# Seven products for eight in three more projections of a two-layer decoder trunk

## The chip, the cores and the metric

The kernel runs as one program on one core of a Trainium2 chip. The metric is the time of one execution on the device, in microseconds (us): the median of several runs. A profiled execution, taken apart, gives the trace.

## The reference, cut to what matters

256 tokens with 2048 features go through two layers. Each layer adds three things to the residual `h`: a mixer, a gated MLP and a gated embedding.

```python
for i in range(DEPTH):                      # 2 layers
    hn = rms_norm(h, mixer_norm[i])
    h = h + (mla_mixer if i == 0 else gdn_mixer)(hn, ...)
    gate, up = split(rms_norm(h, ffn_norm[i]) @ w_gate_up[i])      # 2048 -> 2 x 5632
    h = h + (silu(gate) * up) @ w_down[i]                          # 5632 -> 2048
    e = rms_norm(p[i] @ w_proj[i], ple_norm[i])                    # 256 -> 2048
    h = h + e * sigmoid(rms_norm(h, ple_gate_norm[i]) @ w_gate[i]) # 2048 -> 2048
...
# gdn_mixer (DeltaNet): proj = hn @ w_in, 2048 -> 12352: q 2048, k 2048, v 4096, z 4096, b 32, a 32
#   q, k, v = silu(conv4(...)); q, k l2-normed per head; a chunked gated delta rule per value head
#   (triangular solve inside a chunk, a state carried over the chunks); o = rms_norm(o) * silu(z); o @ w_out
```

All tensors are float32.

## The kernel before

**Tiling.** The 256 tokens are two row tiles (T = 2) of 128. A matrix product runs over blocks of 512 output columns and over k-tiles of 128 input features. The activations stand transposed in SBUF, one k-tile of one row tile being the 128x128 stationary operand; the weights stream past it, 512 columns at a time, into a PSUM bank.

**Precision.** TensorE takes a shortened float32 (F32R). So each operand is split in two: the high part, which is a cast, and the remainder. `products` (lines 312 to 316) issues three matmuls for each product: high x high, high x remainder of the weight, remainder of the activation x high. The remainder of a weight tile is made at run time by `wsplit` (lines 104 to 111): ScalarE casts `raw` to `wh` (L109), VectorE subtracts (`wl`, L110). A weight tile is 128 x (4 k-tiles x 512).

**Buffers.** `wtile` (lines 90 to 97) hands out the weight tiles: three each of `raw`, `wh` and `wl`, and in the FFN two more `raw`, one more `wh` and `wl` from the pool `extra`. A tile takes one whole buffer however much of it is used. Four PSUM banks (`psmm`) hold accumulators of the large products, four others (`pstr`) everything else. The pool `s4p` holds 20 tiles of 128 x 1024 for activations and intermediates.

**Two ways to multiply.** `linear` (lines 294 to 310) is the plain one: for a block of 512 columns, for each group of four k-tiles, load 1 MB, split, 24 matmuls; then `evac` empties the two banks. `seven` (lines 318 to 390) serves the gate/up product of the FFN alone. It takes two column blocks c1 and c2 at once. For the first eight of the 16 k-tiles it treats rows (two row tiles), inner features (two groups of four k-tiles) and columns (two blocks) as a 2x2 by 2x2 matrix product in Winograd's form: seven products of blocks for eight. Each is a "phase" of 4 k-tiles x 3 matmuls. Four sums of weight blocks (VectorE: L346, L356, L363, L372) are split like plain tiles; four sums of activation blocks are made once per norm (`Norm.operands`). The banks A, B, C, D get some parts by copies: B is begun as a copy of A (L351), C is saved as m5 (L353), A as u2 (L360), D = A + m5 (L367). The other eight k-tiles go into the same banks in the plain way.

**Order.** The program is written as one stream; small work (norms, transposes, convolutions, the chunk algebra) stands in generators in the lists `fill` and `back`, and `tick` advances them by one step after each six large matmuls or so. The framework's scheduler then orders each engine's queue by readiness, earlier code first; on the chip each queue runs in that order, and an instruction that waits holds up what is behind it. SP issues the weight loads; a load waits for its `raw` buffer.

**DeltaNet.** First a block of 320 columns (b, a and half of the last gate block), then queries and keys by blocks of 512, each by `project` (lines 790 to 799), with generators `queries` and `keys` behind each; then eight gate blocks (z), during which `lanes`, the triangular solve in small VectorE steps, runs in `back`; then the value blocks, each followed by a `scan` generator, with the output product `w_out` in between.

Of the kernel before, what the change touches and what calls it, by code (L numbers as in the profile page):

```python
# [10 lines left out]
F32 = mybir.dt.float32  # L11
F32R = mybir.dt.float32r
# [7 lines left out]
P = 128  # L20
T = 2
# [17 lines left out]
S4 = 20  # L39
WBUFS = {"raw": 3, "wh": 3, "wl": 3}  # L40
EXTRA = {"raw": 2, "wh": 1, "wl": 1}
NV0 = 1
# [4 lines left out]
P2 = {"mla": 14, "gdn": 8, "ffn": 1, "ple": 6}  # L47
# [15 lines left out]
def trunk(ctx: ExitStack, tc: tile.TileContext, a: dict, out, plan=("mla", "ffn", "ple", "gdn", "ffn", "ple"), first=0):  # L63
# [55 lines left out]
    nc.vector.memset(ones, 1.0)  # L119

# [63 lines left out]
    class Norm:  # L184


        def __init__(self, wcol, sums=False):
            self.wcol, self.x, self.of7 = wcol, [], sums
            self.ss = sm(8, "ss")
# [10 lines left out]
        def parts(self, b):  # L200
            if self.of7 and b < 2:
                self.operands(b)
            else:
                self.x.append(make_xT(lambda t: h[b][:, t, :], gain(self.wcol + 4 * b)))

        def operands(self, b):
# [16 lines left out]
            def split(dh, dl, src):  # L223
                nc.scalar.copy(out=dh, in_=src)
                nc.vector.tensor_sub(out=dl, in0=src, in1=dh.bitcast(F32))

# [21 lines left out]
        def seven(self, name, kk):  # L248
# [45 lines left out]
    def linear(xs, W, kt, blocks, evac, row0=0, need=None, step=4):  # L294

        for bi, (c0, n) in enumerate(blocks):
            ps = [psmm.tile([P, 512], F32, tag="mm", name="mm") for _ in range(T)]
            for k4 in range(0, kt, 4):
# [3 lines left out]
                for kk in range(kn):  # L302
# [4 lines left out]
                    for t in range(T):  # L307
                        products(ps[t], part(xs, k, t), wh, wl, kk, n, k == 0, k == kt - 1)
# [9 lines left out]
    def seven(nrm, W, c1, c2, evac):  # L318


        A, B, C, D = None, None, None, None
# [4 lines left out]
        def phase(ps, x2, w2, start):  # L326
            for kk in range(4):
                xh, xl = x2(kk)
                products(ps, (xh, xl), w2[0], w2[1], kk, 512, start and kk == 0, kk == 3, skip_group_check=True)
                if kk % 2:  # L330
                    tick()

        def op(name):
            return lambda kk: nrm.seven(name, kk)

        def std(q, t):
            return lambda kk: part(nrm.x, 4 * q + kk, t)

        b11, b12 = wload(W, 0, c1), wload(W, 0, c2)
        b21, b22 = wload(W, 512, c1), wload(W, 512, c2)  # L340
        cs = scope["extra"]
        w2 = wsplit(b11)
        A = bank()
        phase(A, op("A11"), w2, True)
        tm = cs.tile([P, 4, 512], F32, tag="tm", name="tm", bufs=1)
        nc.vector.tensor_sub(out=tm, in0=b12, in1=b11)  # L346
        w2 = wsplit(tm)
        C = bank()
        phase(C, op("S1"), w2, True)
        B = bank()  # L350
        nc.scalar.copy(out=B, in_=A)  # L351
        m5 = cs.tile([P, 512], F32, tag="m5", name="m5", bufs=1)
        nc.scalar.copy(out=m5, in_=C)  # L353
        w2 = wsplit(b21)
        phase(B, op("A12"), w2, False)
        nc.vector.tensor_sub(out=tm, in0=b22, in1=tm)  # L356
        w2 = wsplit(tm)
        phase(A, op("S2"), w2, False)
        u2 = cs.tile([P, 512], F32, tag="u2", name="u2", bufs=1)
        nc.scalar.copy(out=u2, in_=A)  # L360
        w2 = wsplit(b22)
        phase(C, op("S4"), w2, False)
        nc.vector.tensor_sub(out=b12, in0=b22, in1=b12)  # L363
        w2 = wsplit(b12)
        phase(A, op("S3"), w2, False)
        D = bank()
        nc.vector.tensor_add(out=D, in0=A, in1=m5)  # L367
        r1, r2 = wload(W, 1024, c1), wload(W, 1024, c2)
        q1 = wsplit(r1)
        until(lambda: len(nrm.x) > 2)  # L370
        phase(B, std(2, 0), q1, False)
        nc.vector.tensor_sub(out=b21, in0=b21, in1=tm)  # L372
        w2 = wsplit(b21)
        phase(A, op("A22"), w2, False)
        q2 = wsplit(r2)
        phase(A, std(2, 1), q1, False)
        phase(C, std(2, 0), q2, False)
        phase(D, std(2, 1), q2, False)
        r1, r2 = wload(W, 1536, c1), wload(W, 1536, c2)
        q1 = wsplit(r1)  # L380
        until(lambda: len(nrm.x) > 3)
        phase(A, std(3, 1), q1, False)
        phase(B, std(3, 0), q1, False)
        evac(0, 1, A, None)
        evac(0, 0, B, None)
        q2 = wsplit(r2)
        phase(C, std(3, 0), q2, False)
        phase(D, std(3, 1), q2, False)
        evac(1, 0, C, u2)
        evac(1, 1, D, None)  # L390
# [6 lines left out]
    def residual(nxt):  # L397
        def evac(bi, c0, n, ps):
            for t in range(T):
                nc.vector.tensor_add(out=h[bi][:, t, :], in0=h[bi][:, t, :], in1=ps[t])  # L400
            if nxt is not None:
                nxt.block(bi, NLAG)
        return evac
# [216 lines left out]
    def ffn(i, nrm, nxt, ahead):  # L620
        wgu, wd = a["ffn_w_gate_up"][i], a["ffn_w_down"][i]
        parts = [range(0, 3), range(3, 6), range(6, 9), range(9, NFF)]
        for pi, js in enumerate(parts):
            mid = []
            for jb in js:
# [3 lines left out]
                def evac_gu(up, t, ps, u2, sg=sg, md=md, mid=mid):  # L629
# [8 lines left out]
                    if t == T - 1:  # L638
                        later(MLAG, lambda: mid.append(make_xT(lambda t: md[:, t, :], None)))

                seven(nrm, wgu, jb * 512, FF + jb * 512, evac_gu)
            if pi == len(parts) - 1 and ahead is not None:
                ahead()
            linear(mid, wd, 4 * len(js), BLK, residual(nxt if pi == len(parts) - 1 else None), row0=js[0] * 512)
# [37 lines left out]
    def ple(i, nrm, nxt, last):  # L682
# [538 lines left out]
```

## Time and profile before

| | |
|---|---|
| median of 3 runs | 2805.37 us (2803.57 to 2805.95) |
| the profiled execution's own time | 2807.84 us |
| its span (first to last instruction) | 2805.8 us |
| TensorE matmuls busy | 2774.5 us, 99% of the span |
| VectorE busy | 1946.2 us, 69% |
| ScalarE busy | 1443.5 us, 51% |
| mean granted TensorE clock | 0.995 of full speed |
| DMA, mean busy share of q1 over 16 engines | 56.4% |

PE is TensorE, DVE VectorE, ACT ScalarE, SP the queue of the loads. A group of instructions is named by its line, engine, operation and tiles; "idle before, <- X" is the time that its engine waited just ahead of it, and for whom.

### The profile page before, as it was taken

How to read it: one execution, taken by the hardware profiler on the slowest of the kernel's cores; microseconds unless marked ns; L12 is line 12 of the kernel's file. 1: busy time of each engine (PE TensorE's matmuls, PEld its weight loads, DVE VectorE, ACT ScalarE, POOL GpSimd, SP SyncE). 2: the span in 40 equal slices, each digit the busy share in tenths (PEclk: the TensorE clock that was granted, in tenths of full speed). 3: DMA queues.
4: the chain of work that ended last, by engine and by line, in shares of the span. 5: the costliest groups of instructions: out<-in, count | busy, mean ns of one | idle time of the engine just before them, and what ended most of it. 6: DMA issues, size and time to landing. Idle time of an engine off the chain costs nothing.

```text
span 2805.8 us, 33510 instructions
## 1 busy us (share of the span) xinstructions
PE 2774.5 (99%) x13609; PEld 2300.1 (82%) x13609; DVE 1946.2 (69%) x1818; ACT 1443.5 (51%) x1517; POOL 161.6 (6%) x254
## 2 busy tenths in 40 slices
PE   8999999999999999999999999999999999999999
PEld 8778888888888888788888888888788888888887
DVE  5675876877867765556774556657985876867764
ACT  6765653654544555645444444444663554554553
POOL 1430000000000000222100000000000000000000
PEclk9999999999999999999999999999999999999999
DMA  7435465565565545666777545546555464655554
GB/s 225 128 115 190 165 246 174 210 210 171 189 225 195 196 154 175 210 223 213 268 247 237 189 150 188 174 159 215 180 207 198 173 232 150 240 195 194 183 171 145
DMA packets 296444, 540.81 MB, mean 193 GB/s; under 512 B 34105, under 2 KB 55266, under 8 KB 296034
## 3 DMA queue, kind: packets, MB, share of 16 engines
q1 hardware_dynamic: 295858, 536.58, 56.4%
q8 instruction: 107, 1.75, 0.3%
q10 hardware_dynamic: 432, 2.10, 0.2%
q14 instruction: 47, 0.39, 0.0%
HBM read 517.63 MB, written 21.00 MB: 192 GB/s over the span
## 4 chain that ended last, share of the span: by engine, by line
PE 50%; DVE 1%; ACT 1%; issue 1%; DMA 0%; POOL 0%; DVEq 0%; ACTq 0%
PE mm L314 15%; PE mm L316 15%; PE mm L315 15%; PE tr L965 1%; PE tr L1074 1%; PE tr L1080 1%; PE tr L155 1%; DVE wl L110 1%; ACT wh L109 0%; DMA raw<-in_ffn_w_gate_up 0%; PE tr L808 0%; PE tr L868 0%; PE tr L1055 0%; DVE vb L1133 0%; POOL r8o L122 0%
## 5 line engine op out<-in xcount | busy, mean ns | idle before, releaser
L110 DVE TENSOR_TENSOR wl<-raw,wh 128x2048 fp32r<-128x2048 f32 (+4 forms) x514 | 1120.7, 2191 | 546.6 <-ACT wh L109 545.6
L314 PE MATMUL mm<-wh,xh 128*128 128x512 f32 (+1 forms) x3600 | 1414.1, 393 | 5.2 <-ACT wh L109 5.1
L316 PE MATMUL mm<-wh,xl 128*128 128x512 f32 (+1 forms) x3600 | 1395.3, 388 | 0.0
L315 PE MATMUL mm<-wl,xh 128*128 128x512 f32 (+1 forms) x3600 | 1392.1, 387 | 0.9 <-DVE wl L110 0.9
L109 ACT CAST wh<-raw 128x2048 fp32r<-128x2048 f32 (+4 forms) x514 | 936.3, 1826 | 741.3 <-PE mm L316 588.6
L314 PEld LDWEIGHTS mm<-wh,xh 128*128 128x128 f32 x3600 | 678.4, 189 | 141.4 <-ACT wh L109 6.7
L316 PEld LDWEIGHTS mm<-wh,xl 128*128 128x128 f32 x3600 | 677.5, 188 | 138.1 <-DVE xl L593 0.2
L315 PEld LDWEIGHTS mm<-wl,xh 128*128 128x128 f32 x3600 | 678.8, 189 | 131.5 <-DVE wl L110 2.2
L109 ACT CAST wh<-tm 128x2048 fp32r<-128x2048 f32 x44 | 84.0, 1909 | 135.9 <-PE mm L316 115.0
L110 DVE TENSOR_TENSOR wl<-tm,wh 128x2048 fp32r<-128x2048 f32 x44 | 100.6, 2286 | 28.7 <-ACT wh L109 28.6
L400 DVE TENSOR_TENSOR h<-h,mm 128x512 f32<-128x512 f32 x104 | 68.8, 682 | 25.0 <-PE mm L316 24.9
L122 POOL TENSOR_TENSOR re<-re,neghalf 128x2 f32<-128x2 f32 x2 | 5.4, 2704 | 1348.0 <-DVE re L672 1348.0
L631 ACT ACTIVATE sg<-mm,rs 128x512 f32<-128x512 f32 x44 | 30.3, 689 | 62.1 <-PE mm L316 62.1
L346 DVE TENSOR_TENSOR tm<-raw 128x2048 f32<-128x2048 f32 x22 | 50.3, 2288 | 14.0 <-DMA raw<-in_ffn_w_gate_up 14.0
L363 DVE TENSOR_TENSOR raw<-raw 128x2048 f32<-128x2048 f32 x22 | 50.3, 2284 | 1.0 <-DMA raw<-in_ffn_w_gate_up 1.0
L356 DVE TENSOR_TENSOR tm<-raw,tm 128x2048 f32<-128x2048 f32 x22 | 50.4, 2292 | 0.7
L372 DVE TENSOR_TENSOR raw<-raw,tm 128x2048 f32<-128x2048 f32 x22 | 50.3, 2285 | 0.2
L164 ACT ACTIVATE xh<-tr,ncol 128x256 fp32r<-128x256 f32 x88 | 38.9, 476 | 22.2 <-PE tr L155 16.0
L816 DVE SCALAR_TENSOR_TENSOR vT<-tr,cw,vT 128x255 f32<-128x255 f32 (+2 forms) x96 | 40.1, 473 | 10.8 <-ACT vT L393 10.6
L165 DVE SCALAR_TENSOR_TENSOR xl<-tr,ncol,xh 128x256 fp32r<-128x256 f32 x88 | 39.4, 479 | 11.6 <-ACT xh L164 10.7
L177 ACT ACTIVATE junk<-h 128x512 f32<-128x512 f32 x48 | 29.9, 626 | 12.9 <-DVE h L400 10.1
L314 PE MATMUL mm<-wh,x 128*128 128x512 f32 x88 | 34.5, 392 | 0.0
(289 smaller groups left out, 1694.1 us busy)
## 6 DMA issues: line engine op xcount, KB each, us to landing
raw<-in_ffn_w_gate_up SPq DMA_DIRECT2D x176, 1024.0 KB, 5.7
raw<-in_gdn_w_in SPq DMA_DIRECT2D x92, 1024.0 KB, 5.3
raw<-in_ffn_w_down SPq DMA_DIRECT2D x88, 1024.0 KB, 5.2
raw<-in_ple_w_gate SPq DMA_DIRECT2D x32, 1024.0 KB, 5.0
raw<-in_gdn_w_out SPq DMA_DIRECT2D x32, 1024.0 KB, 5.2
raw<-in_mla_w_o SPq DMA_DIRECT2D x16, 1024.0 KB, 5.1
raw<-in_mla_w_ukv SPq DMA_DIRECT2D x8, 1024.0 KB, 5.4
raw<-in_mla_w_in SPq DMA_DIRECT2D x8, 768.0 KB, 4.9
```

The lines of the kernel that those rows point to most:

```text
L109: nc.scalar.copy(out=wh[:, k:e, :n], in_=src[:, k:e, :n])
L110: nc.vector.tensor_sub(out=wl[:, k:e, :n], in0=src[:, k:e, :n], in1=wh[:, k:e, :n].bitcast(F32))
L165: nc.vector.scalar_tensor_tensor(out=xl[:, s], in0=ps[:, c:c + n], scalar=w, in1=xh[:, s].bitcast(F32), op0=ALU.mult, op1=ALU.subtract)
L314: mm(ps[:, :n], lhsT=xh, rhs=wh[:, kk, :n], start=start, stop=False, **kw)
L315: mm(ps[:, :n], lhsT=xh, rhs=wl[:, kk, :n], start=False, stop=False, **kw)
L316: mm(ps[:, :n], lhsT=xl, rhs=wh[:, kk, :n], start=False, stop=stop, **kw)
L346: nc.vector.tensor_sub(out=tm, in0=b12, in1=b11)
L356: nc.vector.tensor_sub(out=tm, in0=b22, in1=tm)
L363: nc.vector.tensor_sub(out=b12, in0=b22, in1=b12)
L372: nc.vector.tensor_sub(out=b21, in0=b21, in1=tm)
L400: nc.vector.tensor_add(out=h[bi][:, t, :], in0=h[bi][:, t, :], in1=ps[t])
L816: nc.vector.scalar_tensor_tensor(out=acc[:, o + s:o + 256], in0=src[:, 0:256 - s], scalar=cw[:, jj * 64 + f:jj * 64 + f + 1], in1=acc[:, o ...
```

## The change

`seven` gets a size s: s = 4 is the gate/up product, s = 2 does the first four k-tiles in seven phases of two k-tiles, the other k-tiles plainly. With s = 2 it now also computes the down product (column blocks in pairs), the gate of the embedding and the DeltaNet projections except the 320-column block and the last two gate blocks. The sums of activation blocks for s = 2 come from a class `Half`. The weight sums are made in place in the raw tiles (the tile `tm` is gone), m5 and u2 come from the pool `p2`, and bank C is emptied ahead of the last phase of D. In DeltaNet the projections run in pairs (q0 with k0, ..., gates 0 and 1, gates 2 and 3, values 0 and 1, gates 4 and 5, then values in pairs); gates 6 and 7 move into the value stage. Blocks narrower than 512 columns first get a matmul with a zero matrix over the whole bank.

```diff
-S4 = 20
+S4 = 22
-P2 = {"mla": 14, "gdn": 8, "ffn": 1, "ple": 6}
+P2 = {"mla": 13, "gdn": 9, "ffn": 2, "ple": 6}
...
+            if whole:      # in linear, ahead of the first k-tile
+                for t in range(T):
+                    mm(ps[t].rearrange("p (a c) -> p a c", a=4), lhsT=zero,
+                       rhs=zero.unsqueeze(1).to_broadcast([P, 4, P]), start=True, stop=False)
...
-    def seven(nrm, W, c1, c2, evac):
+    def seven(xs, op, s, W, kt, c1, c2, evac, row0=0, u2col=None):
...
+        if s == 4:
+            b11, b12 = wload(W, row0, c1), wload(W, row0, c2)
+            b21, b22 = wload(W, row0 + 512, c1), wload(W, row0 + 512, c2)
+        else:
+            r1, r2 = wload(W, row0, c1), wload(W, row0, c2)
+            b11, b21, b12, b22 = r1[:, 0:2], r1[:, 2:4], r2[:, 0:2], r2[:, 2:4]
+        A, C, B = bank(), bank(), bank()
+        phase(A, fast("A11"), wsplit(b11, s), s, True)
+        nc.vector.tensor_sub(out=b12, in0=b12, in1=b11)
+        w2 = wsplit(b12, s)
+        phase(C, fast("S1"), w2, s, True)
         nc.scalar.copy(out=B, in_=A)
+        m5, u2 = p2(name="m5"), p2(name="u2")
         nc.scalar.copy(out=m5, in_=C)
+        phase(B, fast("A12"), wsplit(b21, s), s)
         nc.vector.tensor_sub(out=b12, in0=b22, in1=b12)
+        phase(A, fast("S2"), wsplit(b12, s), s)
+        if u2col is None:
+            nc.scalar.copy(out=u2, in_=A)
+        else:
+            scaled(u2, A, u2col)
+        phase(C, fast("S4"), wsplit(b22, s), s)
+        nc.vector.tensor_sub(out=b11, in0=b12, in1=b11)
+        phase(A, fast("S3"), wsplit(b11, s), s)
         D = bank()
         nc.vector.tensor_add(out=D, in0=A, in1=m5)
+        for k in range(2 * s, kt, 4):
+            first, last = k == 2 * s, k + 4 >= kt
+            q1 = wsplit(wload(W, row0 + k * P, c1))
+            raw2 = wload(W, row0 + k * P, c2)
+            until(lambda: len(xs) > k // 4)
+            if first:
+                phase(B, std(k, 0), q1, 4)
+                nc.vector.tensor_sub(out=b21, in0=b21, in1=b12)
+                phase(A, fast("A22"), wsplit(b21, s), s)
+            q2 = wsplit(raw2)
+            phase(A, std(k, 1), q1, 4)
+            if last:
+                evac(0, 1, A, None)
+            if not first:
+                phase(B, std(k, 0), q1, 4)
+            if last:
+                evac(0, 0, B, None)
+            phase(C, std(k, 0), q2, 4)
+            if last:
+                evac(1, 0, C, u2)
+            phase(D, std(k, 1), q2, 4)
+            if last:
+                evac(1, 1, D, None)
...
+        def sums(self, xf):      # class Half
+            self.cut(*self.x, xf)
+            nc.vector.tensor_add(out=f[:, 0], in0=a21, in1=a22)
+            nc.vector.tensor_sub(out=f[:, 1], in0=f[:, 0], in1=a11)
+            nc.vector.tensor_sub(out=f[:, 2], in0=a11, in1=a21)
+            nc.vector.tensor_sub(out=f[:, 3], in0=a12, in1=f[:, 1])
+            s2 = xpair()
+            self.cut(*s2, f.rearrange("p z k c -> p (z k c)"))
...
-            linear(mid, wd, 4 * len(js), BLK, residual(...), row0=js[0] * 512)
+            for b0 in (0, 2):
+                seven(mid, of_half(...), 2, wd, 4 * len(js), b0 * 512, b0 * 512 + 512,
+                      residual2(b0, ...), row0=js[0] * 512)
...
-        linear(nrm.x, a["ple_w_gate"][i], 16, BLK, evac)
+        for b0 in (0, 2):
+            seven(nrm.x, nrm.op, 2, a["ple_w_gate"][i], 16, b0 * 512, b0 * 512 + 512, evac2(b0))
...
-                fill.append(queries(b, project(b * 512), rho, Es))
-                fill.append(keys(b, project(2048 + b * 512), rho, Es))
-            for gg in range(8):
-                linear(nrm.x, W, 16, [(8192 + gg * 512, 512 if gg < 7 else 256)], ...)
-                if gg == 0:
-                    while fill:
-                        tick()
-                    back.append(lanes(lp))
-            first_v = [project(4096 + gg * 512) for gg in range(NV0)]
+                xq, xk = project2(b * 512, 2048 + b * 512)
+                fill.append(queries(b, xq, rho, Es))
+                fill.append(keys(b, xk, rho, Es))
+            gates(0)
+            while fill:
+                tick()
+            back.append(lanes(lp))
+            gates(2)
+            xv = project2(4096, 4608)
+            gates(4)
...
-        for gg in range(8):
-            fill.append(scan(gg, first_v[gg] if gg < NV0 else project(4096 + gg * 512)))
-            if gg in (3, 5):
-                w_out((gg - 3) // 2)
+        for i in range(4):
+            if i:
+                xv = project2(4096 + i * 1024, 4608 + i * 1024)
+            fill.extend(scan(2 * i + c, xv[c]) for c in range(2))
+            if i == 0:
+                continue
+            if i == 1:
+                for gg, n in ((6, 512), (7, 256)):
+                    linear(nrm.x, W, 16, [(8192 + gg * 512, n)], ..., whole=n < 512)
+            if i < 3:
+                w_out(i - 1)
```

## Rows read from the trace of the kernel before

**Rows 1.** The page, part 1: busy us, share and instructions of each engine.
```profile
PE 2774.5 (99%) x13609; PEld 2300.1 (82%) x13609; DVE 1946.2 (69%) x1818; ACT 1443.5 (51%) x1517; POOL 161.6 (6%) x254
```

**Rows 2.** The page, part 4: the chain that ended last, by engine.
```profile
PE 50%; DVE 1%; ACT 1%; issue 1%; DMA 0%; POOL 0%; DVEq 0%; ACTq 0%
```

**Rows 3.** Timeline of TensorE (start us, us, what): first and last of 57 matmuls.
```profile
327.62 0.39 PE L314 MATMUL mm<-wh,xh 128*128 128x512 f32 x1
...
340.31 0.39 PE L316 MATMUL mm<-wh,xl 128*128 128x512 f32 x1
```

**Rows 4.** Windows: stretch us, busy us of engines, granted clock, DMA share, GB/s.
```profile
925.00:980.00 55.00, 54.81 (x246) 44.97 (x246) 38.56 (x32) 30.97 (x36) 1.92 (x1) 1.00 0.70 240
...
1160.00:1300.00 140.00, 133.67 (x632) 111.60 (x631) 82.22 (x119) 73.50 (x72) 41.98 (x45) 0.94 0.66 218
1300.00:1400.00 100.00, 97.18 (x473) 81.47 (x472) 66.61 (x108) 47.40 (x45) 18.98 (x29) 0.98 0.71 239
...
2039.00:2081.00 42.00, 42.00 (x190) 34.66 (x189) 37.36 (x22) 24.74 (x19) 0.00 (x0) 1.00 0.56 201
```

**Rows 5.** The chain in order of time (start us, us, what), behind the last matmul.
```profile
2799.46 1.37 DVE psg L691 x2
```

**Rows 6.** Groups by line and form: xcount | busy us, mean ns | idle before.
```profile
L110 DVE TENSOR_TENSOR wl<-raw,wh 128x2048 fp32r<-128x2048 f32 x466 | 1064.7, 2295 | 493.1 <-ACT wh L109 492.2
L109 ACT CAST wh<-raw 128x2048 fp32r<-128x2048 f32 x466 | 888.7, 1909 | 696.9 <-PE mm L316 546.8 <-DVE h L400 46.3 <-DMA raw<-in_ffn_w_gate_up 42.7
...
L367 DVE TENSOR_TENSOR mm<-mm,m 128x512 f32<-128x512 f32 x22 | 15.2, 691 | 0.0
...
L353 ACT COPY m<-mm 128x512 f32<-128x512 f32 x22 | 12.9, 587 | 5.9 <-PE mm L316 5.9
L351 ACT COPY mm<-mm 128x512 f32<-128x512 f32 x22 | 12.5, 570 | 15.8 <-PE mm L316 12.6 <-DVE md L636 3.2
...
L225 DVE TENSOR_TENSOR xl<-f,xh 128x1024 fp32r<-128x1024 f32 x4 | 4.9, 1218 | 0.0
...
L224 ACT CAST xh<-f 128x1024 fp32r<-128x1024 f32 x4 | 4.2, 1047 | 2.3 <-DVE f L238 2.3
```

**Rows 7.** Timeline of ScalarE and VectorE in the embedding gate, one weight tile.
```profile
1034.24 1.91 ACT L109 CAST wh<-raw 128x2048 fp32r<-128x2048 f32 x1 [3.57 <-PE mm L316]
...
1036.18 2.29 DVE L110 TENSOR_TENSOR wl<-raw,wh 128x2048 fp32r<-128x2048 f32 x1 [3.19 <-ACT wh L109]
```

**Rows 8.** Timeline of VectorE and ScalarE in a gate/up pair.
```profile
334.05 2.29 DVE L363 TENSOR_TENSOR raw<-raw 128x2048 f32<-128x2048 f32 x1
336.25 2.29 DVE L356 TENSOR_TENSOR tm<-raw,tm 128x2048 f32<-128x2048 f32 x1
...
347.16 0.59 ACT L353 COPY m<-mm 128x512 f32<-128x512 f32 x1 [0.29 <-PE mm L316]
```

**Rows 9.** The page, part 6: loads, KB each, median us to landing.
```profile
raw<-in_ffn_w_gate_up SPq DMA_DIRECT2D x176, 1024.0 KB, 5.7
...
raw<-in_ple_w_gate SPq DMA_DIRECT2D x32, 1024.0 KB, 5.0
```

**Rows 10.** Groups by line between 1160 and 1300 us.
```profile
L314 PE MATMUL mm<-wh,xh 128*128 128x512 f32 x158 | 64.4, 408 | 0.0
L316 PE MATMUL mm<-wh,xl 128*128 128x512 f32 x157 | 62.7, 400 | 0.0
L315 PE MATMUL mm<-wl,xh 128*128 128x512 f32 x157 | 62.4, 397 | 0.0
```

**Rows 11.** Timeline of TensorE in the ramp of queries and keys.
```profile
1166.63 3.57 PE L832 MATMUL tr<-ones,sq 128*128 128x1 f32 x16 [3.34 <-ACT sq L827]
```

**Rows 12.** Windows, columns as in rows 4.
```profile
1640.00:1648.00 8.00, 7.29 (x71) 5.62 (x71) 4.99 (x6) 3.71 (x5) 0.00 (x0) 0.79 0.26 103
```

**Rows 13.** Waits between 1640 and 1648 us: in total, times, longest.
```profile
PE tr L965 <- DVE xl L165: 0.7, 1, 0.7
```

More of the change, by code (lines that the diff above doesn't have):

```diff
@@ L119, in trunk @@
     nc.vector.memset(ones, 1.0)
+    zero = const.tile([P, P], F32R, name="zero")
+    nc.scalar.activation(out=zero, in_=ident, func=AF.Copy, scale=0.0)
     def rsqrt_(t, n):
@@ L200, in parts @@
         def parts(self, b):
-            if self.of7 and b < 2:
+            if self.form == 4 and b < 2:
                 self.operands(b)
+            elif self.form == 2 and b == 0:
+                self.half = Half(lambda t: h[b][:, t, :], gain(self.wcol))
+                self.x.append(self.half.x)
             else:
@@ L307, in linear @@
                     for t in range(T):
-                        products(ps[t], part(xs, k, t), wh, wl, kk, n, k == 0, k == kt - 1)
+                        products(ps[t], part(xs, k, t), wh, wl, kk, n, k == 0 and not whole, k == kt - 1)
                     tick()
@@ L330, in phase @@
                 if kk % 2:
                     tick()
[L333 to L350, printed above, removed]
+        def fast(name):
+            return lambda kk: op(name, kk)
+        def std(k0, t):
+            return lambda kk: part(xs, k0 + kk, t)
+        if s == 4:
[4 more added lines that the diff above has]
+            b11, b21, b12, b22 = r1[:, 0:2], r1[:, 2:4], r2[:, 0:2], r2[:, 2:4]
@@ L372, in seven @@
[L372 to L385, printed above, removed]
@@ L392, in scaled, with of_half, op @@
+    def of_half(hold):
+        def op(name, kk):
+            until(lambda: hold() is not None)
+            return hold().op(name, kk)
+        return op
     def scaled(dst, src, col):
@@ L402, in evac, with residual2 @@
                 nxt.block(bi, NLAG)
+        return evac
+    def residual2(b0, nxt):
+        def evac(c, t, ps, u2):
+            z = h[b0 + c][:, t, :]
+            if u2 is not None:
+                nc.vector.tensor_add(out=z, in0=z, in1=u2)
+            nc.vector.tensor_add(out=z, in0=z, in1=ps)
+            if nxt is not None and (c, t) in ((0, 0), (1, 1)):
+                nxt.block(b0 + c, NLAG)
         return evac
@@ L1175, in trunk @@
         last = n == len(steps) - 1
-        nxt = None if last else Norm(WC[kind[steps[n + 1][0]], steps[n + 1][1]], sums=steps[n + 1][0] == "ffn")
+        nxt = None if last else Norm(WC[kind[steps[n + 1][0]], steps[n + 1][1]], {"ffn": 4, "ple": 2, "gdn": 2}.get(steps[n + 1][0]))
         with ExitStack() as ctx:
```

148 lines of the change are left out of this document (92 added, 56 removed).

## The prediction

> **What bounds the kernel now.** The page's first part comes first: TensorE is busy for 2774.5 of 2805.8 us, VectorE for 1946.2, ScalarE for 1443.5 [rows 1]. Then the chain of waits: half of it is put down to TensorE, and no other engine has more than 1% [rows 2]. So TensorE sets the end, nearly everywhere. One run of 57 matmuls between 327.62 and 340.31 us shows the price of one: 12.69 / 56 = 0.2266 us from start to start, while each row says 0.39, because they overlap [rows 3]. The share of VectorE is 59% (1160 to 1300, queries and keys) to 70% (925 to 980, the last down part), and 89% in a gate/up pair, the one place that already takes seven products for eight: 37.36 of 42 us, and TensorE has no gap there [rows 4]. That pair is the yardstick. It is covered by four wh and wl buffers of full size.
>
> **The change, part by part.**
>
> *Matmuls removed.* For the first four k-tiles of a pair of column blocks the plain form takes 4 x 2 x 2 x 3 = 48 matmuls, the seven products take 7 x 2 x 3 = 42. Pairs: down, 4 parts x 2 in each of two FFNs, 16; embedding gate, 2 x 2, 4; DeltaNet, 4 of queries and keys, 3 of gates, 4 of values, 11. 31 pairs x 6 = 186 matmuls x 0.2266 = 42.1 us. Added are four zero matmuls (two blocks narrower than 512): 0.9 us. At the very end the last block's two halves are now evacuated one by one, so that one multiplication of the two behind the last matmul goes: 1.37 / 2 = 0.7 us [rows 5]. Net 41.9 us off TensorE.
>
> *What VectorE and ScalarE get for it.* A full weight tile costs 1.91 us of cast on ScalarE and 2.295 us for the remainder on VectorE; a half one costs 1.05 and 1.22 [rows 6]. In rows back to back the second starts 0.07 to 0.09 earlier; I take 1.14 per half on VectorE. Per pair two full splits become seven half ones and four half subtractions: 11 x 1.14 - 2 x 2.2 = 8.1 us more (a subtraction priced as a remainder) on VectorE, with the D addition (0.69, as L367) and the u2 addition (the same shape) 9.3 to 9.5. ScalarE: 7 x 1.05 - 2 x 1.91 = 3.5, and three copies of 0.57 to 0.59 [rows 6], 5.3. Eleven operand sets of the new class cost VectorE four sums of 512 columns and one more remainder, about 3.5 us each. VectorE in all: 1946 + 31 x 9.4 + 11 x 3.5 = 2276, 81% of the span. As a mean that fits; the question is when.
>
> *The section of seven half phases, outside the FFN.* A phase of a half tile lasts 6 x 0.2266 = 1.36 us, and a wh/wl buffer holds one half tile, whatever its size. There are three of each (the fourth exists in the FFN alone). So a tile can start only when the phase three before it has ended, and it has 2 x 1.36 = 2.72 us to be cast (1.05) and split (1.22): 2.27 if nothing else is in the way. Now, in the plain form, the turn is loose: the cast waits 3.57 us for TensorE to give the buffer back and VectorE waits 3.19 for the cast [rows 7]. What gets in the way, in the order of the two queues: on ScalarE the copy to B stands ahead of the third tile's cast, the m5 copy (it waits for the end of phase S1) ahead of the fourth, the u2 copy (end of S2) ahead of the full tile q1; on VectorE the subtraction b21 - b12 and D = A + m5. The existing pair has such copies between its casts too [rows 8]. Laid out by hand from the start of A11, with 0.17 us for the drain of a phase (0.39 - 0.2266): the third tile is in time; the fourth is ready at 4.37, wanted at 4.3: about 0.1 late; b22 has its buffer at 2.9, is cast from 3.74, split to 6.0, wanted at 5.7: 0.3 late; q1, a full tile, has its buffer at 5.7, the u2 copy ahead of it, is cast 6.4 to 8.3 and split to 10.6, wanted at 8.7: 1.9 late. Sum 2.3 us. Behind q1 the second raw tile is loaded into a buffer free at about 8.3 and lands 5.0 later [rows 9], cast and split to 17.5, wanted at 17.4: just in time. Where VectorE has work of its own inside that stretch it is added. In the embedding gate that is 1.4 us, the multiplication and addition for D of the pair before; beside the gates of DeltaNet it is the triangular solve, some three of its steps. So 3.7 us a pair for 8 pairs with little other TensorE work (4 embedding gate, 3 gates, the first values): 29.6 us. Bounds: 0 (the existing pair has none) and 5.7 (all 3.4 us of an embedding pair's evacuation in the way).
>
> *Queries, keys and the later values*, 7 pairs. TensorE has other work there. Between 1160 and 1300 us there are 472 of the large matmuls [rows 10], 107.0 us; 140 less these, 6.3 idle and 8.4 (0.06 of it) lost to the clock [rows 4] leaves 18 us in 472 / 192 = 2.46 pairs, 7.4 a pair: transposes and products of the chunk algebra, which can run while a weight tile is late, if they are ready. I take 1.4 late per pair, which eats what the pair saves: 9.8 us; ends 0 and 3.7.
>
> *The down product with 12 k-tiles*, 12 pairs: the fourth buffer gives each tile one phase more, 2.3 - 1.36 = 0.9 a pair, 10.8 us; ends 0 and 2.3. *The last part of each FFN* has 8 k-tiles, and the embedding and the next operands beside it. In 925 to 980 VectorE is busy for 38.56 us, TensorE for 54.81 [rows 4]. After: 38.56 + 2 x 9.4 + 3.5 = 60.9 against 54.81 - 2.7 = 52.1. VectorE is the bound by 8.8; half of that can be done beside the neighbours, where it has some room (42 - 37.36 = 4.6 us a pair): 4.3 late per FFN, 8.6 in all; ends 0 and 17.6.
>
> *Edits costed at nothing.* The gate/up pair now subtracts in place, so its four raw tiles live longer, with five raw buffers: cover is the order in which the subtractions already run ahead of their turn, L363 and L356 at 334 and 336 us for phases that come after 346 [rows 8]; if it goes, the first late tile is a raw one whose buffer comes free a phase later: its load (5.7), cast and split (4.2) [rows 6, 9] less three phases of 2.72, 1.7 us, so 0 to 37 us for 22 pairs. More buffers of the s4 pool against two more tiles held per norm and per part cancel. Raw loads are as many as before (8 of 1 MB per pair), on the same queue in the order c1, c2; the write of a gate block goes out one pair later at most and is read by a scan much later. The ramp of DeltaNet has its stalls (below); I leave them as they are, and keep minus 19 and plus 19 as ends.
>
> **The sum.** -41.9 + 29.6 + 9.8 + 10.8 + 8.6 = +16.9 us against the profiled execution's 2807.84 us (its span and 2.0 around it), which lies 2.5 above the median of the runs, 2805.37. I predict 2822 us.
>
> **A rule weighed.** The rows say that half a tile is ready in 2.27 us where a full one takes 4.2 [rows 6]. The Trainium skill (Trace Analysis, "Optimizing Scalar/DVE Operations") says that where Scalar and Vector are not saturated but cause bubbles on other engines, breaking up instructions may let the work finish sooner. By it the half tiles would shorten the waits; it is rival A. No run here shows it yet: the rows have no half tile that is consumed in 1.36 us.
>
> **Rivals.** *A, the cover holds (faster).* The subtractions and first tiles are done ahead, in the long phases of q1 and q2, where VectorE waits 3 us per tile [rows 7], and TensorE finds them ready, as in the gate/up pair at 89% [rows 4]. Lateness nil gives 2805.4 - 41.9 = 2763; half of my 58.8 gives 2793; its centre is 2780. It decides at 41.9 us of lateness in all, 1.35 a pair. Against it: three buffers can't hold more than three half phases, 4.1 us, where the gate/up pair holds four of 2.72.
> *B, even.* The ramp of queries and keys has stalls, one of them 3.34 us for the square behind a cast on ScalarE [rows 11]. TensorE is idle for 6.3 us in 1160 to 1300 and 2.8 in the next 100, and the clock's means, 0.94 and 0.98, lose 0.06 x 140 and 0.02 x 100, 10 us, to stretches at 1.2 GHz [rows 4]: 19 us. With queries and keys starting a pair later the decays could be ready in time: 2822 - 19 = 2803. Against: the chain behind a query block is as long as before.
> *C, the clock (slower still).* Between 1640 and 1648 us a wait of only 0.7 us, beside small products, goes with a mean clock of 0.79: 3.4 us at 1.2 GHz, 1.7 lost [rows 12, 13]. If the gaps in each of the 15 pairs with three buffers do that: 2822 + 25 = 2847.
> That fewer matmuls go than counted would show in the count of records; I give it no chance of its own.
>
> **Chances.** My forecast 0.38 (own range 2812 to 2838), A 0.36, B 0.14, C 0.12. What can be told from no change is 0.2%, 5.6 us. A is faster, B within, the other two slower: 0.36, 0.14, 0.50. The range from 2775 to 2850 leaves out the full gain of A (about 0.1) and the worst of C.
>
> **What would show it.** TensorE's large matmuls fewer by 186 and its busy time near 2733; VectorE near 2276 us. Idle of TensorE 60 us higher, put down to the wl remainder at the start of B with q1 and to b22, in the embedding gate, the gates of DeltaNet and 925 to 980, none in gate/up. Wrong: if those stages have no gaps (A); if the gaps are in gate/up and go to DMA; if the gain is in the ramp.

## The result and the profile after

The changed kernel takes 2906.52 us (median; 2905.17 to 2909.87), the kernel before 2805.66 us on the same chip: a ratio of 1.0361, 95% interval 1.0343 to 1.0379. It is 101 us slower, where 17 us were forecast. The profiled execution has a span of 2904.9 us.

The page's first part and its chain by engine, which answer to [rows 1, 2]:

```profile
PE 2788.7 (96%) x13427; PEld 2273.9 (78%) x13427; DVE 2259.7 (78%) x2197; ACT 1599.3 (55%) x1780; POOL 170.1 (6%) x254
...
PE 79%; DVE 11%; ACT 4%; issue 2%; POOL 2%; DMA 1%; ACTq 0%; SPq 0%; DVEq 0%; POOLq 0%
```

TensorE has 182 instructions fewer, the 186 less 4 that were counted. VectorE's busy time is 2259.7 us, 16 under the forecast. But TensorE is idle for 2904.9 - 2788.7 = 116.2 us, where it was idle for 31.3, and its busy time did not fall to 2733: it rose by 14. VectorE and ScalarE, which had no more than 1% each of the chain, now hold 11 and 4%.

The waits of TensorE over the whole span (in total, times, longest), which had 5.1 us for `wh` and 0.9 for `wl` in the kernel before:

```profile
PE mm L324 <- DVE wl L109: 46.0, 38, 4.1
PE mm L323 <- ACT wh L108: 34.1, 32, 6.1
```

Waits for a weight tile rose from 6.0 to 80.1 us, which is 74.1 of the 84.9 us of new idle time: 70 waits, about 1.1 us each. They lie where the short sections are. The first block is DeltaNet but for its end (1107 to 2039 us), the second the last down part of the first FFN with the embedding behind it (932 to 1107), the third the first FFN up to there, with the mixer's output product before it (225 to 932); nearly all of the other 20 us lie in the second layer's FFN and embedding (17) and at the very start (3.4):

```profile
PE mm L324 <- DVE wl L109: 31.0, 20, 4.1
PE mm L323 <- ACT wh L108: 10.9, 9, 6.1
...
PE mm L323 <- ACT wh L108: 9.9, 10, 2.0
PE mm L324 <- DVE wl L109: 5.8, 5, 1.5
...
PE mm L323 <- ACT wh L108: 2.1, 2, 1.7
PE mm L324 <- DVE wl L109: 0.2, 1, 0.2
```

Not all are VectorE's: 34.1 us are waits for ScalarE's cast. The longest of all, 6.09 us, opens the first pair of queries and keys. There the cast that TensorE needs stands in ScalarE's queue behind three loads of activation tables of 1.28 us each, of which the last is shown:

```profile
1155.74 0.80 PE L323 MATMUL mm<-wh,xh 128*128 128x512 f32 x1 [6.09 <-ACT wh L108]
...
1153.20 1.28 ACT L843 ACT_TABLE_LOAD   x1
...
1154.66 2.92 ACT L108 CAST wh<-raw 128x1024 fp32r<-128x1024 f32 x3
```

The clock took more. Core by core (span, mean granted clock), first before, then after:

```profile
core 0: 2805.8 us, clock 0.995
```

```profile
core 0: 2904.9 us, clock 0.986
```

0.014 x 2904.9 less 0.005 x 2805.8 is 26.6 us more lost to stretches at 1.2 GHz. With 84.9 us of idle that makes 111.5; 41.2 of matmuls go, and the span grew by 99.1, so 28.8 are left over. They are in busy time. Half may be the way the records count it (an estimate): a row lasts 0.39 us where 0.2266 pass from start to start, so each stop of the stream adds some 0.17 us of busy time: 118 stops in the trace of after and 30 before would make 88 x 0.17 = 15 us; the other 14 I could not place.

One late pair in DeltaNet, gates beside the chunk algebra. TensorE:

```profile
1454.98 0.50 PE L323 MATMUL mm<-wh,xh 128*128 128x512 f32 x1 [0.46 <-ACT wh L108]
1459.59 0.79 PE L324 MATMUL mm<-wl,xh 128*128 128x512 f32 x1 [4.10 <-DVE wl L109]
1460.18 0.63 PE L325 MATMUL mm<-wh,xl 128*128 128x512 f32 x1
1460.60 0.63 PE L323 MATMUL mm<-wh,xh 128*128 128x512 f32 x1
...
1469.45 0.50 PE L324 MATMUL mm<-wl,xh 128*128 128x512 f32 x1 [1.83 <-DVE wl L109]
1479.19 0.50 PE L324 MATMUL mm<-wl,xh 128*128 128x512 f32 x1 [2.40 <-DVE wl L109]
```

VectorE in the same stretch:

```profile
1452.20 0.16 DVE L984 TENSOR_SCALAR ssk<-ssk 128x4 f32<-128x4 f32 x1
1456.04 1.23 DVE L1001 TENSOR_TENSOR LT<-tr,E 128x1024 f32<-128x1024 f32 x1 [3.68 <-POOL E L991]
1457.18 1.21 DVE L1001 TENSOR_TENSOR AT<-tr,E 128x1024 f32<-128x1024 f32 x1
1458.32 3.48 DVE L109 TENSOR_TENSOR wl<-raw,wh 128x1024 fp32r<-128x1024 f32 x3
1461.72 1.22 DVE L380 TENSOR_TENSOR raw<-raw 128x1024 f32<-128x1024 f32 x1
...
1476.41 0.52 DVE L1041 TENSOR_TENSOR X<-X,pr 128x350 f32<-128x350 f32 x1
1476.85 2.29 DVE L109 TENSOR_TENSOR wl<-raw,wh 128x2048 fp32r<-128x2048 f32 x1
```

ScalarE and SyncE's queue:

```profile
1453.89 1.05 ACT L108 CAST wh<-raw 128x1024 fp32r<-128x1024 f32 x1
1454.83 0.59 ACT L360 COPY m<-mm 128x512 f32<-128x512 f32 x1
1455.31 1.06 ACT L108 CAST wh<-raw 128x1024 fp32r<-128x1024 f32 x1
...
1470.56 1.91 ACT L108 CAST wh<-raw 128x2048 fp32r<-128x2048 f32 x1 [2.55 <-DMA raw<-in_gdn_w_in]
1474.60 1.91 ACT L108 CAST wh<-raw 128x2048 fp32r<-128x2048 f32 x1 [2.12 <-DMA raw<-in_gdn_w_in]
```

```profile
1463.01 8.51 SPq L100 DMA_DIRECT2D raw<-in_gdn_w_in  x3
```

Three things are to be seen. An instruction of the chunk algebra behind the keys (`LT`, the decay mask times a product) that waits 3.68 us for GpSimd stands in VectorE's queue ahead of three remainders; two of their casts had ended by 1454.9, the third by 1456.4. The next three raw tiles are loaded only from 1463.0 on, and the next casts wait for data, 2.55 and 2.12 us: SyncE's queue was held until 1462.2 by transfers that wait for the same `LT`, and 0.8 us longer by the last in-place sum (L380, to 1462.9), until which the section's raw tiles live. And 5.9 us of triangular solve (to 1476.9) stand ahead of the remainder that TensorE misses by 2.40 us. SyncE's waits, between 1455 and 1475 us, then that for the in-place sum in the whole span and in DeltaNet alone (1133 to 2075 us):

```profile
SPq L1011 <- DVE LT L1001: 4.6, 1, 4.6
...
SPq L100 <- DVE raw L380: 0.8, 1, 0.8
...
SPq L100 <- DVE raw L380: 357.6, 32, 25.7
...
SPq L100 <- DVE raw L380: 21.1, 3, 18.0
```

The wait for L380 is nearly new (before, one wait of 4.5 us for the sum at L346). But only 3 of its 32 places lie in DeltaNet, and 18, 200.4 us, in the first three parts of the two FFNs, where TensorE hardly waits for weights. So it is not shown to be what makes DeltaNet late.

In the last down part it is another limit. Columns as in [rows 4]; the second column pair of the first FFN's last part, then the first pair of the second FFN's:

```profile
1002.00:1017.00 15.00, 8.73 (x30) 5.63 (x29) 14.73 (x18) 11.46 (x14) 0.00 (x0) 0.90 0.20 68
```

```profile
2751.00:2767.00 16.00, 10.53 (x34) 6.67 (x33) 15.23 (x18) 6.84 (x7) 0.18 (x1) 0.89 0.35 107
```

Here VectorE has hardly any idle time (14.73 of 15, 15.23 of 16): half remainders, in-place sums and evacuations meet what is made for the embedding, the new operands in the first row, the scaling of `e` in the second. In the embedding gate itself VectorE has some room (busy for 18.40 of 20 us from 1022, 27.23 of 31 from 1066). There TensorE waits in each of the four pairs where it was forecast to, for the remainder of q1:

```profile
1043.47 0.50 PE L324 MATMUL mm<-wl,xh 128*128 128x512 f32 x1 [1.25 <-DVE wl L109]
...
1095.25 0.50 PE L324 MATMUL mm<-wl,xh 128*128 128x512 f32 x1 [1.49 <-DVE wl L109]
...
2817.16 0.50 PE L324 MATMUL mm<-wl,xh 128*128 128x512 f32 x1 [1.68 <-DVE wl L109]
...
2863.28 0.50 PE L324 MATMUL mm<-wl,xh 128*128 128x512 f32 x1 [1.82 <-DVE wl L109]
```

### The profile page after: what moved, and what is told of

Read it like the earlier page. It is cut to its first block, busy times and chain, and to the rows that moved or that the text cites. A ratio compares the mean times of both kernels' runs of the same rounds, so it can differ in the third digit from the quotient of the medians.

```text
span 2904.9 us, 33968 instructions
## 1 busy us (share of the span) xinstructions
PE 2788.7 (96%) x13427; PEld 2273.9 (78%) x13427; DVE 2259.7 (78%) x2197; ACT 1599.3 (55%) x1780; POOL 170.1 (6%) x254
## 4 chain that ended last, share of the span: by engine, by line
PE 79%; DVE 11%; ACT 4%; issue 2%; POOL 2%; DMA 1%; ACTq 0%; SPq 0%; DVEq 0%; POOLq 0%
PE mm L324 24%; PE mm L323 24%; PE mm L325 24%; DVE wl L109 5%; ACT wh L108 2%; PE tr L1071 1%; PE tr L156 1%; PE tr L1180 1%; PE tr L1186 1%; DVE raw L362 1%; PE S L626 1%; POOL E L991 0%; DVE xl L434 0%; DVE raw L369 0%; DVE raw L380 0%
## 5 line engine op out<-in xcount | busy, mean ns | idle before, releaser
L109 DVE TENSOR_TENSOR wl<-raw,wh 128x2048 fp32r<-128x2048 f32 (+3 forms) x713 | 1339.4, 1895 | 352.6 <-ACT wh L108 351.0
L108 ACT CAST wh<-raw 128x2048 fp32r<-128x2048 f32 (+3 forms) x713 | 1121.6, 1589 | 804.7 <-PE mm L325 512.2
L323 PE MATMUL mm<-wh,xh 128*128 128x512 f32 (+3 forms) x3538 | 1401.9, 398 | 39.8 <-ACT wh L108 34.1
L324 PE MATMUL mm<-wl,xh 128*128 128x512 f32 (+3 forms) x3538 | 1385.5, 392 | 46.7 <-DVE wl L109 46.0
L325 PE MATMUL mm<-wh,xl 128*128 128x512 f32 (+3 forms) x3538 | 1378.9, 390 | 0.0
L355 DVE TENSOR_TENSOR raw<-raw 128x1024 f32<-128x1024 f32 (+1 forms) x53 | 88.2, 1663 | 15.3 <-DMA raw<-in_ffn_w_down 9.9
L369 DVE TENSOR_TENSOR raw<-raw 128x1024 f32<-128x1024 f32 (+1 forms) x53 | 89.8, 1694 | 0.8
L362 DVE TENSOR_TENSOR raw<-raw 128x1024 f32<-128x1024 f32 (+1 forms) x53 | 88.5, 1669 | 1.2
L380 DVE TENSOR_TENSOR raw<-raw 128x1024 f32<-128x1024 f32 (+1 forms) x53 | 88.1, 1662 | 0.3
L468 DVE TENSOR_TENSOR h<-h,mm 128x512 f32<-128x512 f32 x64 | 43.7, 683 | 15.5 <-PE mm L325 15.0
L358 ACT COPY mm<-mm 128x512 f32<-128x512 f32 x53 | 30.5, 575 | 27.1 <-PE mm L325 19.8
L365 ACT COPY u<-mm 128x512 f32<-128x512 f32 x45 | 26.7, 593 | 26.4 <-PE mm L325 26.4
L372 DVE TENSOR_TENSOR mm<-mm,m 128x512 f32<-128x512 f32 x53 | 36.7, 693 | 5.3 <-PE mm L325 5.2
```

Source lines behind the costliest of these rows:

```text
L108: nc.scalar.copy(out=wh[:, k:e, :n], in_=src[:, k:e, :n])
L109: nc.vector.tensor_sub(out=wl[:, k:e, :n], in0=src[:, k:e, :n], in1=wh[:, k:e, :n].bitcast(F32))
L323: mm(ps[:, :n], lhsT=xh, rhs=wh[:, kk, :n], start=start, stop=False, **kw)
L324: mm(ps[:, :n], lhsT=xh, rhs=wl[:, kk, :n], start=False, stop=False, **kw)
L325: mm(ps[:, :n], lhsT=xl, rhs=wh[:, kk, :n], start=False, stop=stop, **kw)
L355: nc.vector.tensor_sub(out=b12, in0=b12, in1=b11)
```

## The experiments

Theory Lead (L in one text): what fails is the look-ahead, counted in tiles. A half tile takes a whole `wh`/`wl` buffer and two raw tiles live for a whole section, so any delay of VectorE reaches TensorE. Rivals: Rate (VectorE's added work itself), the queue (Q: one instruction that waits for GpSimd holds up the remainders behind it), and the order (the new pairs and their ramp). Ratios are to the kernel before; times are medians. Lateness is what a part costs and the matmuls that it saves, added: all that is lost, idle and clock together.

**Which part.** Four kernels undo a part each. e1 keeps only the down products (before's single order in DeltaNet), e2 has plain DeltaNet products in the new order, e3 a plain embedding gate, e5 the new order with no seven products but the old ones of gate/up, in their edited form.

```diff
-            seven(nrm.x, nrm.op, 2, W, 16, c1, c2, evac, u2col=nrm.rs[:, 0:1])
+            plain2(nrm.x, W, 16, c1, c2, evac)      # e2; the gates likewise
-            seven(nrm.x, nrm.op, 2, a["ple_w_gate"][i], 16, b0 * 512, ..., evac2(b0))
+            plain2(nrm.x, a["ple_w_gate"][i], 16, b0 * 512, ..., evac2(b0))      # e3
```

> Seven products in the down product alone; the embedding gate and all of DeltaNet are plain and in the order of the kernel before. Lead (half tiles in three buffers leave too little work in hand): what stays is the FFN's share of the loss, the last parts: 2815 to 2835 us. Order (the new DeltaNet order costs, the sevens don't): 2800 to 2810, as the down product then only saves its 22 us, less little.

> The changed kernel with DeltaNet's projections plain but still in pairs and in the new order. Lead: DeltaNet gets back most of its 54 us, 2850 to 2865. Order: it gets back little, 2885 or more.

> The changed kernel with the embedding gate plain. Lead: some 20 to 25 us come back over the two layers, 2880 to 2888. If the last down part of each FFN is what costs there, and not the gate: under 10 us, 2897 or more.

> The new DeltaNet order (projections and gates in pairs, gates 6 and 7 in the value stage) with no seven products beyond gate/up: down, embedding gate and DeltaNet plain. If the stage times of the two earlier runs add, the order alone gains 15 to 20 us: 2785 to 2792. If the gain in DeltaNet there came from something else: 2800 to 2810.

| | us | ratio, 95% interval |
|---|---|---|
| e1 | 2834.15 | 1.0099, 1.0082 to 1.0115 |
| e2 | 2834.53 | 1.0098, 1.0083 to 1.0113 |
| e3 | 2895.73 | 1.0316, 1.0300 to 1.0331 |
| e5 | 2810.61 | 1.0021, 1.0011 to 1.0031 |

e5 is 5 us slower than the kernel before, at the edge of its second expectation, but that is not the order's doing, as far as the traces tell. From the end of the 320-column block to the end of the fourth pair of queries and keys, the ramp, it is faster; before, then e5 (columns as in [rows 4]):

```profile
1125.00:1347.00 222.00, 212.73 (x1003) 177.03 (x1001) 135.58 (x201) 119.65 (x121) 59.53 (x61) 0.95 0.67 220
```

```profile
1129.00:1334.00 205.00, 201.07 (x973) 167.50 (x972) 124.47 (x186) 121.63 (x117) 59.69 (x61) 0.98 0.68 226
```

TensorE's idle time falls from 9.3 to 3.9 us and the clock's loss from about 11 to 4. Most of it comes back later: by the last writes of `h`, all of DeltaNet takes 877.7 us for 881.4. The two FFNs, where e5 has the edited gate/up product, take 5.1 us more. So the edit of gate/up and the order are not separated by a run of their own.

The DeltaNet pairs cost 72 us (2906.5 - 2834.5), more than the 54 that e2's text expected, and save 66 matmuls, 15.0 us: 87 us of lateness, 7.9 a pair. Half of it lies in the four pairs of queries and keys; the change, then e2, which has the same order:

```profile
1149.00:1393.00 244.00, 212.93 (x947) 171.10 (x946) 165.97 (x229) 130.57 (x140) 66.13 (x61) 0.92 0.57 190
```

```profile
1148.00:1353.00 205.00, 201.57 (x975) 168.15 (x974) 125.03 (x186) 122.39 (x120) 63.65 (x61) 0.98 0.68 226
```

They take 39 us more and save 5.4: 44 of lateness, 11 a pair. TensorE's idle time is 31.1 us for 3.4, and the clock loses about 15 us more. The first two pairs of gates take 114 us for 96: 10 a pair.

The embedding gate's four pairs cost 10.8 us beside 5.4 saved, 4.1 a pair; that falls between the two expectations of e3. The down products cost 28 us alone and save 96 matmuls, 21.8 us: 50 us of lateness, in which the edit of gate/up is contained.

**How much look-ahead.** e4 splits every `wh` and `wl` buffer into two of two k-tiles, in the same bytes, and with it each full cast and remainder (`wsplit` then hands out half tiles; not printed); e10 gives a fourth raw tile, for which the pool `s4p` gives up two, and leaves the `wh`/`wl` pairs as they were; e7 does both, with all 31 pairs in place. e14 cuts the full casts and remainders in two as e4 does, but leaves the buffers.

```diff
-S4 = 22
-WBUFS = {"raw": 3, "wh": 3, "wl": 3}
-EXTRA = {"raw": 2, "wh": 1, "wl": 1}
+S4 = 20                                  # e10, e7
+WBUFS = {"raw": 4, "wh": 6, "wl": 6}     # e7; e4 with "raw": 3; e10 with "wh": 3, "wl": 3
+EXTRA = {"raw": 2, "wh": 2, "wl": 2}     # e4, e7
-    def wsplit(src, kn=4, n=512, step=4):
+    def wsplit(src, kn=4, n=512, step=2):      # e14, linear likewise
```

> The changed kernel with wh and wl in six buffers of two k-tiles for three of four (four more halves in the FFN's two extra): same SBUF, but a half tile takes half a buffer; each full tile is split in two halves, 0.15 us more on each engine. Lead by wh/wl: the look-ahead in a section doubles, most waits for wl go, 2820 to 2850. Lead by raw tiles or by VectorE's rate: little, 2880 to 2910.

> The changed kernel with six half buffers of wh and wl, a fourth raw tile everywhere and 20 s4 tiles for 22. Raw tiles bind once the half buffers are there: 20 us or more under the 2847 of half buffers alone, 2815 to 2830. VectorE's rate or its queue binds: 2840 to 2855.

> The changed kernel with four raw weight tiles (S4 20) instead of three, and the split pairs at their old full size. If the two reserves add up, the fourth raw tile is worth here what it was worth beside half-size pairs (38 us): 2860 to 2875. If the split pairs bind first and the raw tile only after them (a chain of two, of which the shorter one counts): 2895 to 2907. Rate theory (VectorE's work itself): no change, 2903 to 2910.

> The changed kernel with every cast and remainder cut into instructions of two k-tiles, the buffers as they were (three pairs of four k-tiles, three raw tiles). If the half-size pairs helped by their number (a half tile no longer takes up a whole buffer): 2895 to 2910. If by finer casts (the first half is ready sooner, small VectorE work gets in between): 2845 to 2865.

| | us | ratio, 95% interval | against after |
|---|---|---|---|
| e14, casts cut in two | 2875.71 | 1.0249, 1.0235 to 1.0263 | -31 |
| e4, and twice as many half buffers | 2846.57 | 1.0140, 1.0123 to 1.0157 | -60 |
| e10, fourth raw tile alone | 2892.76 | 1.0316, 1.0301 to 1.0330 | -14 |
| e7, half buffers and fourth raw tile | 2808.91 | 1.0019, 1.0009 to 1.0028 | -98 |

e7 keeps every pair and is within 0.3% of the kernel before. Its page and its two waits:

```profile
PE 2748.0 (98%) x13427; PEld 2264.6 (81%) x13427; DVE 2291.7 (82%) x2661; ACT 1673.7 (60%) x2244; POOL 175.5 (6%) x254
```

```profile
PE mm L334 <- ACT wh L117: 10.5, 10, 3.5
PE mm L335 <- DVE wl L118: 10.0, 7, 1.8
...
SPq L100 <- DVE raw L391: 229.4, 17, 22.0
```

VectorE does 32 us more than in the changed kernel and TensorE waits a quarter as long for weights (20.5 us for 80.1). As a sum over the span, Rate is excluded. Each reserve is worth more beside the other: the raw tile 14 us alone and 38 beside half buffers, which fell between both expectations of e10 for the first and past that of e7 for the second. e14 also fell between its two expectations: of the 60 us of e4, 31 come from finer instructions and 29 more from the number of buffers. So my theory, which had only the number, was half of it. The Trainium skill (Perfetto Trace Analysis, "Optimizing Scalar/DVE Operations") says that breaking up instructions may let work finish sooner where Scalar and Vector aren't saturated but cause bubbles elsewhere; e14 agrees, 31 us, though VectorE and ScalarE are busy for 31 and 42 us longer in it.

**VectorE's work and queue.** e8 leaves out the weight sums of the small product (its products get unsummed weights). e9 issues the products of the chunk algebra that wait for GpSimd three ticks later (e9's text puts them in the scan; they stand behind the keys).

```diff
-        nc.vector.tensor_sub(out=b12, in0=b12, in1=b11)
+        if s == 4:
+            nc.vector.tensor_sub(out=b12, in0=b12, in1=b11)      # e8, the other three likewise
-KY = 3
+KY = 6      # e9
```

> The changed kernel without the four weight subtractions of each pair with s = 2 (left out: the products get unsummed weights); 4.6 us of VectorE per pair gone, 141 in all, and raw tiles free earlier. VectorE's rate binds: 2906 falls by 60 us or more. Lead binds: only the one subtraction that stands inside the section counts, and the rest waits as before: by 15 to 40 us.

> The changed kernel, with the products of the scan that wait for GpSimd's decay mask (LT, AT) issued six ticks later instead of three, nothing else changed. Theory Q (a VectorE instruction that waits for GpSimd holds up the weight remainders queued behind it): its eight waits sum to 24 us in the run with half-size pairs, so 2880 to 2895. Theory L (too few tiles of look-ahead is what makes every delay count, this wait being only one of many): 2895 to 2908.

e8 takes 2856.01 us, 1.0189 (1.0175 to 1.0203): 139 us less VectorE work (2120.4 busy) gave 50 us back. That lies between both theories, and it does not separate them, because the sums also stand at the head of each tile's chain and free the raw tiles. e9 takes 2917.42 us, 1.0399 (1.0383 to 1.0415), 11 us slower than the change and outside both expectations. VectorE's waits for GpSimd:

```profile
DVE LT L1001 <- POOL E L991: 19.2, 7, 3.8
```

The waits hardly moved (24.1 us in 8 before the edit; TensorE's for `wl` 42.4 us for 46.0), so the edit did not take the suspect away and excludes little. Why it costs 11 us stays open. e7 says more: the same instruction waits just as long there,

```profile
DVE LT L1012 <- POOL E L1002: 22.1, 8, 3.5
```

and between 1398 and 1414 us, around one of these waits, TensorE loses 1.8 us to `wl` where the changed kernel lost 4.1 at such a place. At this place the blocked queue is real, and dear where nothing is held in reserve.

**Is the reserve worth as much to plain products, and what do the pairs earn with it?** e13 is the kernel before with half buffers and the fourth raw tile (in the FFN five as it had, where the others have six). e6 is e5 with half buffers and seven products in the first three down parts of each FFN. e12 has both reserves, before's single order and those down parts alone (with the edited gate/up product). e15 is e12 in the new order, and e11 is e15 with the DeltaNet pairs.

```diff
+                if pi == len(parts) - 1:      # e6, e11, e12, e15: the last down part plain
+                    plain2(mid, wd, 4 * len(js), b0 * 512, b0 * 512 + 512, ...)
+                    continue
```

> As the kernel with the order alone, plus seven products in the first three down parts of each FFN (12 of the 31 pairs), with wh and wl in six half buffers. Lead: with the look-ahead doubled the 12 pairs keep most of their 16 us: 8 to 14 us under the order alone. If the down pairs lose what they save: the same or above.

> The kernel before with half-size split pairs and four raw tiles (five in the FFN, as it had), no product changed. Look-ahead theory, for sevens: plain products consume a whole tile over 16 k-tile groups and their reserve sufficed (31 us of TensorE idle in all), so little to gain: 2795 to 2806. If look-ahead is worth as much to plain products, the reserve and not the products made the fastest run: 2778 to 2790.

> Half-size split pairs and four raw tiles in the order of the kernel before, with seven products only in the first three down parts of each FFN; DeltaNet, embedding gate and last down parts plain. 12 pairs save 90 matmuls (20.4 us) and the stages of the profile gave back 4 us per FFN with full-size pairs. Look-ahead theory: 2792 to 2800. If the fewer scratch tiles (S4 20) cost the scan: 2800 to 2810.

> Half-size split pairs and four raw tiles, seven products kept in the DeltaNet projections and in the first three down parts of each FFN, plain products in the embedding gate and in the last down part. Look-ahead theory: with both reserves the DeltaNet pairs earn their 15 matmuls each (11 pairs, 37 us) less what the half phases still cost; against the run with every pair (2808.9) the last parts and embedding gates gain about 3 us each: 2796 to 2803. Rate theory (short phases cost wherever they stand): the pairs taken out only give up their saved matmuls, 2808 to 2818.

> Half-size split pairs and four raw tiles, the new order with plain products in DeltaNet, the embedding gate and the last down parts, seven products in the first three down parts. Against the run that differs by the DeltaNet sevens alone (2801.2): if they earn all their 165 matmuls with the reserve, 2830 to 2838; if they only break even, 2798 to 2804; if they still cost, 2775 to 2790 (the 20 us of the down parts under the 2810.6 of the plain order, less what the reserve gives).

The matmul counts in the last three of these texts are too high by my slip: a pair saves 6, so 12 down pairs save 72 (16.3 us) and 11 DeltaNet pairs 66 (15.0 us), as the records show (13541 and 13475, against 13609, with the four zero matmuls added).

| | us | ratio, 95% interval |
|---|---|---|
| e6 | 2806.37 | 1.0009, 1.0000 to 1.0018 |
| e13 | 2801.63 | 0.9989, 0.9980 to 0.9997 |
| e12 | 2780.56 | 0.9916, 0.9902 to 0.9929 |
| e15 | 2786.96 | 0.9933, 0.9920 to 0.9947 |
| e11 | 2801.20 | 0.9989, 0.9981 to 0.9998 |

The reserve alone is worth 3.5 us to plain products (e13), against 98 to the changed kernel. It serves the short sections. With it the twelve down pairs of e12 earn 21 us over e13, all of their 16 and 5 more. By the last writes of `h` in the two traces, 19.0 us apart, the six parts with these pairs are 16.1 us shorter and the last parts 3.0 longer; the other 6.1 lie in DeltaNet, whose products are the same, and why is not shown. e6, which lacks the fourth raw tile, was only 4 under e5, where 8 to 14 were expected. e12 came out 11 us under the lower end of what was expected of it. The DeltaNet pairs still cost: e11 is 14 us behind e15 and has 15.0 us of matmuls less, so 29 us of lateness remain, 2.7 a pair. The two from within the embedding gate, plain in both, into DeltaNet's last products, first e11, then e15 (columns as in [rows 4]):

```profile
1066.00:1945.00 879.00, 853.50 (x4825) 706.14 (x4824) 649.59 (x941) 474.14 (x598) 99.40 (x108) 0.99 0.59 202
```

```profile
1065.00:1929.00 864.00, 856.02 (x4886) 716.11 (x4885) 554.32 (x841) 442.32 (x546) 96.77 (x108) 1.00 0.61 205
```

With the pairs VectorE is busy for 95 us more there, TensorE for 2.5 less: it is idle for 25.5 us instead of 8.0. All pairs against none in the last down part and embedding gate cost 7.7 us (e7 less e11).

e12 beats both kernels: 24.6 us under the kernel before. Its page:

```profile
PE 2752.2 (99%) x13541; PEld 2281.5 (82%) x13541; DVE 2116.7 (76%) x2476; ACT 1595.7 (57%) x2128; POOL 167.6 (6%) x254
```

## Why the prediction was wrong

It had the sign, and the mechanism as far as it went (a short section outruns three buffers), and missed the size: 17 us forecast, 101 measured, outside its range.

- *Matmuls removed.* Right in number: 13427 records for 13609.
- *VectorE's work.* Right: 2259.7 us for 2276; a half remainder takes 1.229 us and a half sum 1.22 to 1.27.
- *Embedding gate, 3.7 a pair.* Right in size, 4.1 by e3, and in place: the remainder of q1 comes 1.25 to 1.82 us late in the four pairs, where the layout had 1.9.
- *Gate/up at nothing.* Nearly: the first FFN up to its last part waits 2.3 us for weights, and in e5 its first three parts are 2.3 us longer than before.
- *The step that failed in DeltaNet: the price from the layout by hand, 3.7 a pair, and above all the cover that took it to 1.4 in queries, keys and later values.* 24.6 us were forecast for 11 pairs, 87 measured. Queries and keys: 1.4 a pair forecast, 11 measured. TensorE's other work there was to run while a tile is late; it did not cover (31.1 us idle), and nearly all of the rest of that stage's loss is the clock's. The first two gate pairs: 3.7 forecast, 10 measured. The layout counted `wh` and `wl` buffers alone and let each engine reach a tile as soon as its input was there. In the trace 3.68 us of waiting for GpSimd and 5.9 us of solve stand ahead of remainders, where three steps of the solve had been allowed for, and table loads ahead of a cast (6.09 us). Raw tiles came late too: from 1133 to 1670 us casts wait 30.3 us in 14 places for a load. How much each of these is worth, no run separates. With both reserves 2.7 a pair are left (e11 against e15), near the forecast's mean of 2.2 only in the sum: in queries and keys e11 takes 222 us for e15's 209, about 4.6 a pair, and 1.5 are left for each of the others.
- *The step that failed in the down product: the last part of each FFN, 4.3.* 12 pairs at 0.9 and 4.3 per last part make 19.4 us; e1 measured 50. By the last writes of `h` in the changed kernel, the first three parts of both FFNs are 5.9 us shorter than before, so 10.4 of the 16.3 us saved were lost: 0.9 a pair, as forecast. The two last parts are 15.3 and 14.5 us longer: 35 us of lateness, 17.6 each. The forecast took 925 to 980 us for the last part; those rows hold mostly the last gate/up pair and the embedding's first product. The part's columns run from 973 to 1018, before:

```profile
973.00:1018.00 45.00, 45.00 (x211) 37.33 (x211) 34.33 (x40) 25.40 (x37) 5.07 (x5) 1.00 0.52 176
```

The same sum from this row is 34.33 + 2 x 9.4 + 3.5 = 56.6 for VectorE against 45 - 2.7 = 42.3, an excess of 14.3 (an estimate), near what came. Giving half of it to the neighbours was wrong as well: e1 has a plain embedding gate behind the part, and its last parts are still 13.8 and 11.8 us longer.

- *Rival A* failed as made, and its cover can be had for twelve pairs (e12). *Rival B* came true in part: the ramp gains some 12 of its 19 us (e5), but most of it is lost again behind it. *Rival C* came true in its price, 26.6 us for 25, and together with my forecast instead of in its place: both come from the same gaps, and I should have put it into the sum. In part that was luck: some 7 us of it lie in the last down parts, which C did not count.

Sum of lateness by part: 87 + 16 + 50 and the 5 of e5, less 42, is 116 where 101 were measured; the parts share some of it, the edit of gate/up in both e1 and e5 for one.

## What to carry to other kernels

When a change shortens the work per tile, count the look-ahead anew for every stage of the tile's way (raw tile, cast, remainder) and in time of consumption, with what else stands in each in-order queue. A buffer scheme that is loose for long tiles says nothing of short ones: here the same reserve was worth 3.5 us to the old form and 98 to the new. And when gaps are forecast, put the clock's loss into the sum with them.

## What the runs showed that was not expected

The clock fell with waits as short as these. In the pair shown above TensorE stood for 0.46 us and, one matmul later, for 4.10; then it ran at 1.2 GHz, half the full clock, while VectorE caught up. Matmuls start 0.42 us apart there (1460.18, 1460.60) instead of 0.2266:

```profile
1457.70:1464.50 6.80, 4.91 (x12) 3.85 (x13) 6.46 (x6) 1.04 (x1) 0.00 (x0) 0.50 0.77 248
```

And the two reserves are not additive: 60 us for the half buffers and 14 for the raw tile alone, 98 for both.
